# A two-layer hybrid trunk on one core: the layer head in parts behind weight splits, the spatial gating in two parts inside branch C

## The chip, the cores and the metric

The kernel runs on one core of one Trainium2 chip. Its engines are TensorE (PE), VectorE (DVE), ScalarE (ACT), GpSimd (POOL) and SyncE (SP); each works through its own queue in order. The metric is the device time of one execution in microseconds (us). Three runs of the kernel before took 1119.67, 1120.45 and 1121.61 us, median 1120.45. A time differs from that measurably from about 0.2% on, some 2.2 us.

## The reference

Input x is 512 tokens by 1024. Two layers, each a parallel mixer, then a final RMSNorm:

```
h    = rmsnorm(x, norm_g)
proj = h @ w_in            # aq ak av az | u vb | bz | cq ck cv cz | gl
A: 4 heads, differential causal attention; rmsnorm; * silu(az)
B: vb = layernorm(gelu(vb)); u = gelu(u)
   mixed = tril(sgu_w) applied to vb in chunks of 128 tokens, per group, + sgu_b
   yb = u * mixed * silu(bz)
C: 8 heads, three dilated windows merged by their log-sums; * silu(cz)
x    = x + (sum over branches of sigmoid(gl) * (y @ w_branch)) @ w_out
```

All is float32. The kernel keeps that precision by splitting: each operand is a high half (rounded) plus a low half, and a product is three matmuls (high by high, high by low, low by high).

## The kernel before, in words

Activations lie transposed, features on the partitions: `xh`/`xl` are the two halves of the normalised x, 8 tiles (kc) of 128 by 512. Weights stream from memory as `raw` tiles of 512 KB on SP's queue (two buffers). Each half of a `raw` tile is split: ScalarE rounds it to `whi` (L160), VectorE, or every fifth time GpSimd, takes the rest as `wlo` (L161). There are six `whi` and five `wlo` buffers. `proj_T` (L398 to L400) and `proj_M` (L423 to L425) consume them; a pair of outputs not listed in `EIGHT` goes by a scheme of seven products of half size (`seven`), which needs sums of weights (L180 to L183) and differences of x's blocks, `mh`/`ml` (`mixes`).

TensorE's memory holds two projection banks `ps_pj`, one double bank `ps_s` for scores, and four `ps_to` for transposes and products with the values.

`plan()` gives the order of the dense items of a layer: `vb`, `val A`, `val C`, `split`, `mix`, `pp A 0` (the head), then the items pulled while attention A runs, then those for attention C, then gates (`gl2`), branch products (`pb`) and the output. `vb` and the two `val` run on the unnormalised x (`xuh`, `xul`), with the norm applied to their outputs. Meanwhile in the head x is scaled (L556, eight VectorE instructions issued at once in `vb`), split to `xh`/`xl` (`split`, half of the low parts on GpSimd) and mixed (`mix`); the gelu and the statistics of `vb` also stand there. `pp A 0` is the first item that needs `xh`/`xl`.

While attention runs, its function calls `fill()` at fixed points, which pulls as much from the dense stream as a budget from `cost()` allows; `need()` forces an item that attention waits for. Scores (L828) of one step go into `ps_s`; VectorE subtracts and takes the maximum (L840), ScalarE exponentiates (L844) and normalises (L862), TensorE transposes (L868), the transposes are split (L403, L404) and multiplied with the values (L974). Each head has three steps (blocks 0 and 1, 2, 3). The spatial gating (`sgu`, L641 to L665) comes after attention C. Its weights `sgw` are loaded on ScalarE's queue. A scheduler fixes every engine's order at build time; weight splits and scores get high priority there.

Of the kernel before, what the change touches and what calls it, by code (L numbers as in the profile page):

```python
# [99 lines left out]
def hybrid_kernel(ctx: ExitStack, tc, xT, posr, wpack, tabs, cvec, pvec, rvec, lamv, sguw, outT):  # L100
# [366 lines left out]
    def mixes(blocks):  # L467

        for h in range(2):
            b11, b12, b21, b22 = blocks(h)  # L470

            def t2(tag, bufs=2):
                return t2k(tag, bufs, name="tm").rearrange("p (k c) -> p k c", k=2)

            m1, m2, m3, m4 = t2("t1"), t2("ob"), t2("sh"), t2("z", 5)
            V.tensor_tensor(out=m1, in0=b12, in1=b11, op=ALU.subtract)
            G.tensor_tensor(out=m3, in0=b22, in1=b12, op=ALU.subtract)
            V.tensor_tensor(out=m2, in0=b22, in1=m1, op=ALU.subtract)
            G.tensor_tensor(out=m4, in0=b21, in1=m2, op=ALU.subtract)
            for i, m in enumerate((m1, m2, m3, m4)):  # L480
                split(mh[:, i, 2 * h : 2 * h + 2, :], ml[:, i, 2 * h : 2 * h + 2, :], m)
# [46 lines left out]
    def layer(l, xu, parts):  # L528
# [13 lines left out]
        def i_vb():  # L542
# [18 lines left out]
            yield from proj_M(banks, xu.pair, {1: norm_sum, 4: scale})  # L561
            rst = norm["rst"]
            mv = sm.tile([P, 4, 2], F32, tag="mv", bufs=1, name="mv")
            rv = sm.tile([P, 4, 1], F32, tag="rv", bufs=1, name="rv")
            for tb in range(4):
                o = vb[:, tb, :]
                A.activation(out=o, in_=banks[tb], func=AF.Copy, scale=rst[:, tb : tb + 1])
# [550 lines left out]
```

## Time and profile before

| | before |
|---|---|
| median of three runs | 1120.45 us |
| profiled execution, whole | 1120.12 us |
| its span in the trace | 1118.4 us |
| TensorE busy | 1087.5 us, 97% |
| VectorE busy | 821.1 us, 73% |
| ScalarE busy | 597.5 us, 53% |
| GpSimd busy | 494.3 us, 44% |

The profiled execution's time exceeds its span by 1.7 us (start and end outside the trace) and lies 0.33 us below the median. Busy shares are averages over the whole span; what bounds a stage is read from the timeline and the waits of that stage. A matmul's duration overlaps the next one's, so the step from start to start tells its price. "[7.30 <-DVE wlo L161]" behind a row says that the engine was idle for 7.30 us before it and that VectorE's `wlo` at line 161 released it.

### The profile page before, as it was taken

The page shows a single profiled execution, that of the slowest core. Times are in us where ns is not written, and L with a number is a line of the kernel's source. Part 1 is how long each engine was busy: PE and PEld are TensorE (multiplying, and loading weights), DVE is VectorE, ACT ScalarE, POOL GpSimd, SP SyncE. Part 2 cuts the span into 40 slices and gives each one's busy share as a digit, 9 for nine tenths or more (in the row PEclk, how much of TensorE's full clock was granted, in tenths as well). Part 3 has the DMA queues.
Part 4 walks back from the last instruction along what each step waited for, and adds up shares of the span by engine and source line. Part 5 has one row for each costly group of instructions (what it writes and reads, how often), then busy time and mean ns, then how long its engine had stood idle before and what let it go on. Part 6 is the DMA issues. An engine that isn't in the chain of part 4 may idle for free.

```text
span 1118.4 us, 17917 instructions
## 1 busy us (share of the span) xinstructions
PE 1087.5 (97%) x6444; PEld 939.0 (84%) x6444; DVE 821.1 (73%) x1500; ACT 597.5 (53%) x1281; POOL 494.3 (44%) x438
## 2 busy tenths in 40 slices
PE   7799999999999999999999999999999999999996
PEld 5688888878888999998888888888788889999886
DVE  7775788566869888874559578885778797878643
ACT  6654565566765444443546546564758644444330
POOL 3312534432525756663334235525243357657431
PEclk9999999999999999999999999999999999999998
DMA  6243131221213323333622413122202132333433
GB/s 205 76 132 95 40 110 60 95 76 38 76 48 104 101 92 111 102 115 105 230 90 76 132 38 114 59 93 76 74 29 87 57 95 95 101 109 94 139 121 99
DMA packets 35064, 105.97 MB, mean 95 GB/s; under 512 B 4704, under 2 KB 7776, under 8 KB 34976
## 3 DMA queue, kind: packets, MB, share of 16 engines
q1 hardware_dynamic: 29936, 98.50, 27.9%
q10 hardware_dynamic: 5040, 6.34, 1.9%
q8 instruction: 51, 0.84, 0.3%
q14 instruction: 37, 0.30, 0.1%
HBM read 100.58 MB, written 4.24 MB: 94 GB/s over the span
## 4 chain that ended last, share of the span: by engine, by line
PE 84%; DVE 9%; DMA 2%; issue 2%; ACT 2%; POOL 1%; POOLq 0%; SPq 0%; DVEq 0%; ACTq 0%
PE ps_pj L398 15%; PE ps_pj L399 14%; PE ps_pj L400 14%; PE ps_to L398 8%; PE ps_to L399 8%; PE ps_to L400 8%; PE ps_s L828 3%; PE ps_to L868 2%; DVE wlo L161 2%; PE ps_to L974 2%; PE ps_to L425 2%; PE ps_to L423 2%; PE ps_to L424 2%; DMA raw<-in_wpack 2%; DVE xf L556 1%
## 5 line engine op out<-in xcount | busy, mean ns | idle before, releaser
L160 ACT ACTIVATE whi<-raw 128x512 fp32r<-128x512 f32 x316 | 193.1, 626 | 236.1 <-DMA raw<-in_wpack 106.8
L161 DVE TENSOR_TENSOR wlo<-raw,whi 128x512 fp32r<-128x512 f32 x261 | 220.2, 852 | 112.9 <-ACT whi L160 41.8
L398 PE MATMUL ps_pj<-xh,whi 128*128 128x512 f32 (+1 forms) x544 | 208.3, 383 | 1.1 <-DVE r L848 0.6
L400 PE MATMUL ps_pj<-xh,wlo 128*128 128x512 f32 (+1 forms) x544 | 205.9, 378 | 0.0
L399 PE MATMUL ps_pj<-xl,whi 128*128 128x512 f32 (+1 forms) x544 | 204.0, 375 | 0.0
L161 POOL TENSOR_TENSOR wlo<-raw,whi 128x512 fp32r<-128x512 f32 x55 | 78.6, 1429 | 129.0 <-ACT whi L160 32.5
L398 PEld LDWEIGHTS ps_pj<-xh,whi 128*128 128x128 f32 x544 | 102.5, 188 | 22.2 <-issue 3.7
L400 PEld LDWEIGHTS ps_pj<-xh,wlo 128*128 128x128 f32 x544 | 102.6, 189 | 17.9 <-issue 1.0
L399 PEld LDWEIGHTS ps_pj<-xl,whi 128*128 128x128 f32 x544 | 102.5, 189 | 17.8 <-issue 1.7
L161 DVE TENSOR_TENSOR wlo<-t,whi 128x512 fp32r<-128x512 f32 x88 | 91.4, 1056 | 21.1 <-ACT whi L160 18.4
L160 ACT ACTIVATE whi<-t 128x512 fp32r<-128x512 f32 x112 | 65.4, 624 | 57.8 <-DVE t L181 42.4
L398 PE MATMUL ps_to<-mh,whi 128*128 128x256 f32 x320 | 91.2, 285 | 1.8 <-ACT whi L160 1.3
L844 ACT ACTIVATE pr<-pr,nm 128x128 f32<-128x128 f32 (+3 forms) x128 | 70.6, 553 | 39.8 <-DVE nm L840 39.8
L400 PE MATMUL ps_to<-mh,wlo 128*128 128x256 f32 x320 | 90.4, 283 | 0.1
L399 PE MATMUL ps_to<-ml,whi 128*128 128x256 f32 x320 | 90.5, 283 | 0.0
L441 POOL TENSOR_TENSOR rsh<-rsh,sinr 128x512 f32<-128x512 f32 x32 | 42.0, 1311 | 105.5 <-DVE rsh L439 101.9
L840 DVE CUSTOM_DVE_ANT_0 pr<-ps_s,tab 128x128 f32<-128x128 f32 (+3 forms) x128 | 56.2, 484 | 22.1 <-PE ps_s L828 17.0
L400 PE MATMUL ps_to<-xh,wlo 128*128 128x256 f32 x240 | 67.9, 284 | 2.3 <-DVE wlo L161 2.1
L398 PE MATMUL ps_to<-xh,whi 128*128 128x256 f32 x240 | 67.9, 283 | 0.3 <-ACT whi L160 0.3
L399 PE MATMUL ps_to<-xl,whi 128*128 128x256 f32 x240 | 67.8, 283 | 0.0
L398 PEld LDWEIGHTS ps_to<-mh,whi 128*128 128x128 f32 x320 | 61.3, 192 | 3.7 <-ACT whi L160 2.4
L400 PEld LDWEIGHTS ps_to<-mh,wlo 128*128 128x128 f32 x320 | 61.2, 192 | 0.5 <-DVE wlo L161 0.3
(241 smaller groups left out, 2854.1 us busy)
## 6 DMA issues: line engine op xcount, KB each, us to landing
raw<-in_wpack SPq DMA_DIRECT2D x174, 512.0 KB
xf<-in_xT SPq DMA_DIRECT2D x8, 256.0 KB
xr<-in_xT ACTq DMA_DIRECT2D x8, 256.0 KB
x1d<-xf SPq DMA_DIRECT2D x8, 256.0 KB
raw<-in_wpack SPq DMA_DIRECT2D x4, 256.0 KB
xr<-x1d ACTq DMA_DIRECT2D x4, 256.0 KB
xr<-x1d ACTq DMA_DIRECT2D x8, 128.0 KB
out<-xf SPq DMA_DIRECT2D x8, 128.0 KB
```

What stands on the lines that cost most here:

```text
L160: A.activation(out=hi, in_=src, func=AF.Copy)
L161: (G if made[0] % LOMOD == 0 and made[0] > FIRST_G else V).tensor_tensor(out=lo, in0=src, in1=hi.bitcast(F32), op=ALU.subtract)
L398: T.matmul(ps, lhsT=wh, rhs=mh, start=first, stop=False)
L399: T.matmul(ps, lhsT=wh, rhs=ml, start=False, stop=False)
L400: T.matmul(ps, lhsT=wl, rhs=mh, start=False, stop=last)
L423: T.matmul(banks[tb], lhsT=mh_[:, ts], rhs=wh, start=kc == 0, stop=False)
L424: T.matmul(banks[tb], lhsT=ml_[:, ts], rhs=wh, start=False, stop=False)
L425: T.matmul(banks[tb], lhsT=mh_[:, ts], rhs=wl, start=False, stop=kc == KC - 1)
L441: G.tensor_tensor(out=sh, in0=sh, in1=sinr, op=ALU.mult)
L828: T.matmul(pss[:, m, at[i]], lhsT=q[HALF[m], a, qs], rhs=k[HALF[m], b, :W], start=t == 0, stop=t == 2,)
L840: V.tensor_tensor_reduce(out=o, in0=pss[:, m, at[i]], in1=tab[:, 0 if br == BR_A else 1, S - W :], op0=ALU.add, op1=ALU.min, scale=-0.125, ...
L844: A.activation(out=o, in_=o, func=AF.Exp, scale=-1.0, bias=nm[:, m : m + 1], accum_out=den[:, m : m + 1],)
```

## The change

Five things change. (1) The scaling and splitting of x is done one kc at a time after each kc of `val A`, the mixing after each kc of `val C`, each queued behind the newest weight split (`behind_weights`), all subtractions on VectorE. (2) `vb`'s gelu and statistics leave the head: four items `vbg` stand between the end of attention A's items and the middle of C's, `vbn` after `pp C 2`. (3) The lambda constants are computed at the end of layer 0's last mix; the loads of the gating weights stand behind weight splits in branch C. (4) `sgu` is split into `sgu 0` and `sgu 2`, inside C's items, uses `ps_pj` and writes back to `uz`; after C an item `yb` only splits the result. (5) There are six `wlo` buffers, and the last layer's sums of squares of the right half are on VectorE.

```diff
-    start = [("vb",), ("val", BR_A), ("val", BR_C), ("split",), ("mix",), ("pp", BR_A, 0)]
-    ... + [("vbn",), ("u2", 2), ("bz2", 0), ("pp", BR_C, 0)]
-    c = [("pp", BR_C, i) for i in range(1, 6)] + [("bz2", 2)]
+    start = [("vb",), ("val", BR_A), ("val", BR_C), ("pp", BR_A, 0)]
+    a += [("u2", 2), ("vbg", 0), ("bz2", 0), ("vbg", 1), ("pp", BR_C, 0), ("vbg", 2)]
+    c = [("pp", BR_C, 1), ("vbg", 3), ("pp", BR_C, 2), ("vbn",), ("sgu", 0), ("pp", BR_C, 3), ("bz2", 2), ("pp", BR_C, 4)]
+    c += [("sgu", 2), ("pp", BR_C, 5)]
-    end = gl[:1] + [("after", "C"), ("sgu",)] + gl[1:2]
+    end = gl[:1] + [("after", "C"), ("yb",)] + gl[1:2]
...
+    def behind_weights():
+        with tc.issue_after(newest[0]), tc.issue_after(newest[1]):
+            yield
...
-            lo = wp.tile([P, S], F32R, tag="wlo", bufs=NSLOT - 1, name="wlo")
+            lo = wp.tile([P, S], F32R, tag="wlo", bufs=NSLOT, name="wlo")
...
-                (V if kc == KC - 1 or self.first else G).tensor_tensor(out=self.ss[:, c], ...
+                (V if kc == KC - 1 or self.first or c.start else G).tensor_tensor(out=self.ss[:, c], ...
...
-                for kc in range(KC):
-                    xsc = xu.f[kc // 2][:, kc % 2, :]
-                    V.scalar_tensor_tensor(
-                        out=xsc, in0=xsc, scalar=ng[:, l, kc : kc + 1], in1=rbc, op0=ALU.mult, op1=ALU.mult
-                    )
...
-                gelu2(o, o)
-                V.bn_stats(out=st[:, tb, :], in_=o)
-                V.bn_aggr(out=mv[:, tb, :], in_=st[:, tb : tb + 1, :])
...
+        def prepare(kc):
+            with behind_weights():
+                xsc = xu.f[kc // 2][:, kc % 2, :]
+                V.scalar_tensor_tensor(
+                    out=xsc, in0=xsc, scalar=ng[:, l, kc : kc + 1], in1=norm["rbc"], op0=ALU.mult, op1=ALU.mult
+                )
+                if kc:
+                    split_x(kc - 1)
+        def mix(kc):
+            with behind_weights():
+                if kc == 0:
+                    split_x(KC - 1)
+                    norm["mix"] = mixes(xu.f)
+                next(norm["mix"])
+                if kc == KC - 1:
+                    next(norm["mix"])
+                    if l == 0:
+                        lambdas()
...
+        def i_sgu(g0):
+            vb, uz = sgu["vb"], sgu["uz"][g0 // 2]
+            if g0 == 0:
+                with behind_weights():
+                    nc.scalar.dma_start(out=sgw[0], in_=rvec[l : l + 1, :].partition_broadcast(P))
+                    nc.scalar.dma_start(out=sgw[1], in_=sguw[l])
...
+                pw = ps_pj()
+                T.matmul(pw, lhsT=ones, rhs=sgw[1], start=True, stop=True)
...
+            for i in range(2):
+                pm = ps_pj()
...
+                    out=uz[:, i, :], in0=ob, scalar=0.25, in1=uz[:, i, :], op0=ALU.mult, op1=ALU.mult
...
+        def i_yb():
+            for i in range(2):
+                split(yhl[BR_B][0][i], yhl[BR_B][1][i], sgu["uz"][i])
...
-            flat = {"vbn": 0.0}
+            flat = {"vbn": 0.0, "vbg": 0.0, "sgu": 2.0}
```

In the rows of order that follow, `xf` is x before the split, `tm` a difference of its blocks, `ml` and `xl` low halves.

VectorE's queue in layer 0's head, before, from the eight scalings on:

```order
L556 SCALAR_TENSOR_TENSOR xf<-xf,pv,rbc 128x512 x8
L569 BN_STATS st<-vb 128x6
L462 SCALAR_TENSOR_TENSOR vb<-gth,vb 128x512
L460 SCALAR_TENSOR_TENSOR gw<-gw,vb 128x512 x2
L404 TENSOR_TENSOR xl<-xf,xh 128x512 x3
L161 TENSOR_TENSOR wlo<-raw,whi 128x512
L404 TENSOR_TENSOR xl<-xf,xh 128x512
L570 BN_AGGR mv<-st 128x2
L161 TENSOR_TENSOR wlo<-raw,whi 128x512
L569 BN_STATS st<-vb 128x6
```

VectorE's queue in the same head now, from the last scaling on (the last kc of `val A` and the first of `val C`):

```order
L588 SCALAR_TENSOR_TENSOR xf<-xf,pv,rbc 128x512
L416 TENSOR_TENSOR xl<-xf,xh 128x512
L172 TENSOR_TENSOR wlo<-raw,whi 128x512
L497 TENSOR_TENSOR tm<-xf 128x512
L416 TENSOR_TENSOR xl<-xf,xh 128x512
L172 TENSOR_TENSOR wlo<-raw,whi 128x512
L497 TENSOR_TENSOR tm<-xf 128x512
L416 TENSOR_TENSOR ml<-tm,mh 128x512
L172 TENSOR_TENSOR wlo<-raw,whi 128x512
L497 TENSOR_TENSOR tm<-xf,tm 128x512
L416 TENSOR_TENSOR ml<-tm,mh 128x512
```

What stood in one go, the eight scalings and the gelu's steps ahead of the next `wlo`, now stands one kc at a time between the `wlo` of the weights, and the gelu and the statistics are not there.

TensorE's queue in layer 0's attention C, before, at head 1's first scores (blocks 0 and 1):

```order
L828 MATMUL ps_s<-k,q 128x128 x6
L828 MATMUL ps_s<-k,q 128x256 x6
L398 MATMUL ps_pj<-xh,whi 128x512
L399 MATMUL ps_pj<-xl,whi 128x512
L400 MATMUL ps_pj<-xh,wlo 128x512
L398 MATMUL ps_pj<-xh,whi 128x512
```

The same place now, from the last matmul of `pp C 2` on (`sgw` by `ones` is the gating's row sum, `sgw` by `vb` its product):

```order
L412 MATMUL ps_pj<-xh,wlo 128x512
L1010 MATMUL ps_to<-pth,vs 128x256
L1010 MATMUL ps_to<-ptl,vs 128x256
L1010 MATMUL ps_to<-pth,vs 128x256
L1010 MATMUL ps_to<-ptl,vs 128x256
L904 MATMUL ps_to<-ident,pr 128x128 x6
L864 MATMUL ps_s<-k,q 128x128 x6
L864 MATMUL ps_s<-k,q 128x256 x6
L671 MATMUL ps_pj<-sgw,ones 128x512
L685 MATMUL ps_pj<-sgw,vb 128x128 x4
L864 MATMUL ps_s<-k,q 128x384 x6
L904 MATMUL ps_to<-ident,pr 128x128 x8
```

Matmuls of a dense item stood behind the scores; now only attention's own work and `sgu 0` stand there.

ScalarE's queue at that place now (`th` reads the bank that `pp C 2` fills last):

```order
L880 ACTIVATE pr,den<-pr,nm 128x512 x2
L171 ACTIVATE whi<-raw 128x512
L664 DMA sgw<-in_rvec 128x512
L462 ACTIVATE th<-ps_pj 128x512
L665 DMA sgw<-in_sguw 128x512
L898 ACTIVATE pr<-pr,rd 128x512 x2
```

The load of the gating weights stands behind `th`; before it stood at the start of the program for layer 0.

TensorE's queue at head 3's last scores, before:

```order
L828 MATMUL ps_s<-k,q 128x512 x6
L868 MATMUL ps_to<-ident,pr 128x128 x3
L398 MATMUL ps_pj<-xh,whi 128x512
L399 MATMUL ps_pj<-xl,whi 128x512
L400 MATMUL ps_pj<-xh,wlo 128x512
L398 MATMUL ps_pj<-xh,whi 128x512
L399 MATMUL ps_pj<-xl,whi 128x512
L400 MATMUL ps_pj<-xh,wlo 128x512
L398 MATMUL ps_pj<-xh,whi 128x512
L974 MATMUL ps_to<-pth,vs 128x256
L399 MATMUL ps_pj<-xl,whi 128x512
L400 MATMUL ps_pj<-xh,wlo 128x512
```

The same place now (`mh` by `whi` is a piece of `gl A 0`, a gate by seven products):

```order
L864 MATMUL ps_s<-k,q 128x512 x6
L1010 MATMUL ps_to<-pth,vs 128x256
L1010 MATMUL ps_to<-ptl,vs 128x256
L1010 MATMUL ps_to<-pth,vs 128x256
L1010 MATMUL ps_to<-ptl,vs 128x256
L1010 MATMUL ps_to<-pth,vs 128x256
L904 MATMUL ps_to<-ident,pr 128x128 x3
L1010 MATMUL ps_to<-ptl,vs 128x256
L1010 MATMUL ps_to<-pth,vs 128x256
L1010 MATMUL ps_to<-ptl,vs 128x256
L904 MATMUL ps_to<-ident,pr 128x128 x3
L410 MATMUL ps_pj<-mh,whi 128x256
```

Dense matmuls of the eight-product kind stood between the instructions of attention; those (`bz2 2`, `gl B 0`) now come ahead of head 3's scores, and behind them only pieces of `gl A 0` are left.

## Rows read from the trace of the kernel before

**Rows 1.** The page: busy time of each engine over the span (share, instructions), and the chain that ended last by engine.

```profile
PE 1087.5 (97%) x6444; PEld 939.0 (84%) x6444; DVE 821.1 (73%) x1500; ACT 597.5 (53%) x1281; POOL 494.3 (44%) x438
...
PE 84%; DVE 9%; DMA 2%; issue 2%; ACT 2%; POOL 1%; POOLq 0%; SPq 0%; DVEq 0%; ACTq 0%
```

**Rows 2.** Busy microseconds of each engine in stretches of 10 us: stretch, its length, then PE, PEld, DVE, ACT, POOL (instructions in brackets), the granted TensorE clock (PEclk), DMA share, GB/s.

```profile
50.00:60.00 10.00, 3.52 (x8) 2.81 (x9) 10.00 (x14) 2.48 (x5) 3.48 (x3) 0.72 0.17 52
310.00:320.00 10.00, 10.00 (x67) 8.29 (x66) 7.07 (x23) 8.44 (x23) 3.75 (x6) 1.00 0.17 54
340.00:350.00 10.00, 8.30 (x66) 7.69 (x65) 9.94 (x19) 6.07 (x12) 3.71 (x2) 1.00 0.39 130
350.00:360.00 10.00, 8.99 (x67) 8.15 (x66) 10.00 (x13) 5.77 (x12) 6.34 (x4) 1.00 0.35 116
610.00:620.00 10.00, 9.59 (x43) 7.62 (x42) 7.93 (x14) 7.30 (x12) 4.54 (x3) 1.00 0.44 125
890.00:900.00 10.00, 7.97 (x49) 6.34 (x50) 10.00 (x16) 4.08 (x8) 4.05 (x3) 1.00 0.26 77
```

**Rows 3.** PE's waits over the whole span: what waited, for whom, us in total, times, longest.

```profile
PE ps_pj L425 <- DVE wlo L161: 7.3, 1, 7.3
```

**Rows 4.** TensorE's timeline at the head of layer 0, from the first matmul of `val A` (33.16) to the first of `pp A 0` (87.44): start, duration, engine, line, operation, tiles, shape, count, and in brackets the idle time before with its releaser.

```profile
33.16 0.39 PE L423 MATMUL ps_pj<-whi,xuh 128*128 128x512 f32 x1
33.39 0.39 PE L424 MATMUL ps_pj<-whi,xul 128*128 128x512 f32 x1
...
56.48 1.22 PE L425 MATMUL ps_pj<-wlo,xuh 128*128 128x512 f32 x2 [7.30 <-DVE wlo L161]
57.51 0.63 PE L425 MATMUL ps_s<-wlo,xuh 128*128 128x512 f32 x1
57.93 0.63 PE L423 MATMUL ps_s<-whi,xuh 128*128 128x512 f32 x1
...
60.92 0.57 PE L423 MATMUL ps_s<-whi,xuh 128*128 128x512 f32 x1
...
87.44 0.39 PE L398 MATMUL ps_pj<-xh,whi 128*128 128x512 f32 x1
```

**Rows 5.** VectorE's timeline in the same place.

```profile
40.49 8.51 DVE L556 SCALAR_TENSOR_TENSOR xf<-xf,pv,rbc 128x512 f32<-128x512 f32 x8
...
53.95 1.88 DVE L404 TENSOR_TENSOR xl<-xf,xh 128x512 fp32r<-128x512 f32 x3
55.75 0.68 DVE L161 TENSOR_TENSOR wlo<-raw,whi 128x512 fp32r<-128x512 f32 x1
```

**Rows 6.** VectorE by line and form between 33 and 62 us: count, busy us, mean ns of one, idle before.

```profile
L161 DVE TENSOR_TENSOR wlo<-raw,whi 128x512 fp32r<-128x512 f32 x6 | 4.0, 678 | 1.4 <-ACT whi L160 1.4
...
L404 DVE TENSOR_TENSOR xl<-xf,xh 128x512 fp32r<-128x512 f32 x4 | 2.6, 678 | 0.0
...
L476 DVE TENSOR_TENSOR tm<-xf 128x512 f32<-128x512 f32 x2 | 1.4, 676 | 0.0
```

**Rows 7.** TensorE's timeline at the end of branch C, in layer 0 (348 and 355) and layer 1 (899).

```profile
348.44 0.39 PE L400 MATMUL ps_to<-xh,wlo 128*128 128x256 f32 x1 [1.43 <-DVE wlo L161]
...
355.81 0.38 PE L398 MATMUL ps_to<-mh,whi 128*128 128x256 f32 x1 [0.99 <-ACT whi L160]
...
899.28 0.73 PE L398 MATMUL ps_pj<-yB,whi 128*128 128x512 f32 x2 [0.92 <-ACT yB L403]
```

**Rows 8.** The loading of layer 1's gating weights: its issue on ScalarE's queue, and the mask on GpSimd that waits for it.

```profile
359.06 0.33 ACTq L632 DMA_DIRECT2D sgw<-in_sguw  x1
...
361.72 0.86 POOL L636 TENSOR_SCALAR_AFFINE_SELECT sgw<-sgw 128x512 f32<-128x512 f32 x1 [3.25 <-DMA sgw<-in_sguw]
```

**Rows 9.** ScalarE in branch C by line between 225 and 345 us (columns as in rows 6; four heads): exponentials (L844) with their sums, normalising (L862), the high halves of the transposes (L403), and by form the `th` of a gate (L450).

```profile
L844 ACT ACTIVATE pr<-pr,nm 128x128 f32<-128x128 f32 (+3 forms) x32 | 17.6, 551 | 4.8 <-DVE nm L840 4.8
...
L862 ACT ACTIVATE pr<-pr,rd 128x128 f32<-128x128 f32 (+3 forms) x32 | 16.1, 552 | 2.6 <-DVE rd L848 2.6
L403 ACT ACTIVATE pth<-ps_to 128x128 fp32r<-128x128 f32 (+3 forms) x32 | 12.9, 430 | 8.2 <-PE ps_to L868 5.7 <-POOL ptl L952 2.3
L844 ACT ACTIVATION_READ_ACCUMULATOR pr<-pr,nm 128x1 f32 x32 | 6.0, 187 | 0.0
...
L450 ACT ACTIVATE th<-ps_pj 128x512 f32<-128x512 f32 x5 | 2.9, 582 | 0.0
```

**Rows 10.** TensorE in branch C: twelve matmuls of scores, and eight of 128 columns, in one go each.

```profile
310.96 0.96 PE L828 MATMUL ps_s<-k,q 64*128 64x128 f32 x12
...
352.58 1.05 PE L655 MATMUL ps_s<-sgw,vb 128*128 128x128 f32 x8
```

**Rows 11.** The first 30 us: two idle times of TensorE, and the loading of a function table on ScalarE.

```profile
19.68 0.49 PE L423 MATMUL ps_to<-whi,xuh 128*128 128x512 f32 x1 [0.55 <-ACT whi L160]
...
23.01 1.19 PE L425 MATMUL ps_to<-wlo,xuh 128*128 128x512 f32 x4 [1.22 <-DVE wlo L161]
...
23.80 1.28 ACT L350 ACT_TABLE_LOAD   x1
```

**Rows 12.** The end of the program: the last sum of squares on GpSimd and the matmul that waits for it.

```profile
1108.24 0.72 POOL L276 TENSOR_TENSOR ssum<-ssum,sq 128x256 f32<-128x256 f32 x1 [4.55 <-ACT sq L272]
...
1109.02 0.38 PE L375 MATMUL ps_s<-ones,ssum 128*128 128x1 f32 x2 [1.00 <-POOL ssum L276]
```

More of the change, by code (lines that the diff above doesn't have):

```diff
@@ L1 @@
 import math
-from contextlib import ExitStack
+from functools import partial
+from contextlib import ExitStack, contextmanager
 import concourse.bass as bass
@@ L275, in square @@
                     return
-                (V if kc == KC - 1 or self.first else G).tensor_tensor(out=self.ss[:, c], in0=self.ss[:, c], in1=sq[:, c], op=ALU.add)
+                (V if kc == KC - 1 or self.first or c.start else G).tensor_tensor(out=self.ss[:, c], in0=self.ss[:, c], in1=sq[:, c], op=ALU.add)
         def pair(self, kc):
@@ L465, in hybrid_kernel, with mixes, rest @@
     LT, RT = slice(0, 256), slice(256, 512)
-    def mixes(blocks):
-        for h in range(2):
[L470 to L481, printed above, removed]
+    def mixes(xf):
+        todo = []
+        def rest():
+            for h, i, m in todo:
+                split(mh[:, i, 2 * h : 2 * h + 2, :], ml[:, i, 2 * h : 2 * h + 2, :], m)
+            todo.clear()
+        for h in range(2):
+            a, b = xf[h], xf[2 + h]
+            b11, b12, b21, b22 = a[:, :, LT], a[:, :, RT], b[:, :, LT], b[:, :, RT]
+            m1, m2, m3, m4 = (
+                t2k(tag, bufs, name="tm").rearrange("p (k c) -> p k c", k=2)
+                for tag, bufs in (("t1", 2), ("ob", 2), ("sh", 2), ("z", 5))
+            )
+            for i, m, x1, x2 in ((0, m1, b12, b11), (2, m3, b22, b12), (1, m2, b22, m1), (3, m4, b21, m2)):
+                V.tensor_tensor(out=m, in0=x1, in1=x2, op=ALU.subtract)
+                rest()
+                todo.append((h, i, m))
+                yield
+        rest()
+        yield
     def seven(bank=ps_to):
@@ L560, in i_vb @@
             banks = [ps_to() for _ in range(4)]
[L561 to L562 removed]
+            yield from proj_M(banks, xu.pair, {1: norm_sum, 4: spread})
             mv = sm.tile([P, 4, 2], F32, tag="mv", bufs=1, name="mv")
             rv = sm.tile([P, 4, 1], F32, tag="rv", bufs=1, name="rv")
+            sgu["norm"] = st, mv, rv
             for tb in range(4):
[L566 to L570 removed]
@@ L571, in i_vb @@
-            V.tensor_scalar(out=rv, in0=mv[:, :, 1:2], scalar1=4.0 * EPS, scalar2=None, op0=ALU.add)
-            G.tensor_tensor(out=rv[:, :, 0], in0=rv[:, :, 0], in1=mhalf, op=ALU.pow)
-            sgu["norm"] = mv, rv
-        def i_split():
-            for kc in range(KC):
-                split(xh[:, kc, :], xl[:, kc, :], xu.f[kc // 2][:, kc % 2, :], G if kc in XLG else V)
-            return
-            yield
-        def i_mix():
-            def blocks(h):
-                a, b = xu.f[h], xu.f[2 + h]
-                return a[:, :, LT], a[:, :, RT], b[:, :, LT], b[:, :, RT]
-            mixes(blocks)
-            return
-            yield
+                A.activation(out=vb[:, tb, :], in_=banks[tb], func=AF.Copy, scale=norm["rst"][:, tb : tb + 1])
@@ L654, in i_sgu @@
                 for tb in range(4):
                     T.matmul(
[L656 to L657 removed]
+                        pm[:, tb * P : (tb + 1) * P], lhsT=vb[:, tb, gs], rhs=wc[:, gs], start=True, stop=True
                     )
@@ L675, in i_val @@
                 banks = [ps_pj(), ps_pj(), ps2[:, 0, :], ps2[:, 1, :]]
-                yield from proj_M(banks, xu.pair, {})
+                yield from proj_M(banks, xu.pair, {kc: partial(prepare, kc) for kc in range(KC)})
                 for tb in range(4):
@@ L682, in i_val @@
             banks = [ps_to() for _ in range(4)]
-            yield from proj_M(banks, xu.pair, {})
+            yield from proj_M(banks, xu.pair, {kc: partial(mix, kc) for kc in range(KC)})
             val[br] = v = att.tile([P, 4, 8, P], F32R, tag="vs", name="vs")
@@ L802, in layer @@
         fns = {
-            "vb": i_vb, "split": i_split, "mix": i_mix, "vbn": i_vbn, "after": i_after, "u2": i_u2, "bz2": i_bz2, "sgu": i_sgu, "val": i_val, "pp": i_pp, "gl2": i_gl2, "pb": i_pb, "out": i_out,
+            "vb": i_vb, "vbg": i_vbg, "vbn": i_vbn, "after": i_after, "u2": i_u2, "bz2": i_bz2, "sgu": i_sgu, "yb": i_yb, "val": i_val, "pp": i_pp, "gl2": i_gl2, "pb": i_pb, "out": i_out,
         }
```

83 lines of the change are left out of this document (44 added, 39 removed).

## The prediction

> **What bounds the kernel now.** First the page: TensorE is busy for 1087.5 of 1118.4 us and carries 84% of the chain that ended last [rows 1]. The matmuls that the change leaves are the same ones (the same products of the same sizes), so it can only win or lose in the 30.9 us in which TensorE is idle and in the stretches at its lower clock. Second, busy time by stretch, to find these places: 50 to 60 us has 3.52 busy and a granted clock of 0.72; 340 to 360 lacks 1.70 and 1.01 us, together 2.71; 890 to 900 lacks 2.03; 610 to 620 lacks 0.41 [rows 2]. Third, TensorE's waits name the largest: 7.3 us at once for a `wlo` of VectorE [rows 3]. Fourth, the timeline there. VectorE has scaled x for 8.51 us from 40.49 on and then does gelu and splits until 55.75, when the awaited `wlo` comes up [rows 5]; TensorE starts again at 56.48, and its matmuls step by 0.42 us until about 60.9, against 0.23 at 33.16 [rows 4]. So the lower of the two clock levels (1.2 GHz) is granted behind the gap of 7.30 us: the price of the gap goes on for 4.4 us after it. Behind the gaps of 1.43 and 0.99 us in branch C [rows 7] the clock stays at 1.00 [rows 2].
>
> **The change part by part. Layer 0's head.** From the first matmul of `val A` (33.16) to the first of `pp A 0` (87.44) it takes 54.28 us [rows 4]. In between stand 2 x 96 matmuls; at 0.23 they take 44.2. The difference of 10.1 us is what can go: 7.3 of idle time, some 2.0 of lower clock (4.4 us in which steps of 0.42 do the work of 0.23), the rest small. Does the new order remove it? For each kc TensorE has 12 matmuls, 2.76 us. VectorE has a `wlo`, a scaling and an `xl` or a `wlo`, a `tm` and an `ml`: three instructions of about 0.68 [rows 6], 2.05 us. ScalarE has two, of some 0.6 by an instruction of the same size [rows 9]. Both keep up, and the order puts each `wlo` ahead of the additions that could delay it, with six split weights in advance. The late one next would be the last mix, ahead of `pp A`'s seven-product relatives only, which come later. What weighs on this is the duration: the eight scalings took 8.51 us, 1.06 each [rows 5], where those `wlo`s and `tm`s that ran beside an idle GpSimd took 0.68. In the new order GpSimd has no subtraction in the head, so I take 0.68; the other end is a rival below. The Trainium skill ("SBUF — State Buffer", section "SBUF: two separate sides") says that a VectorE instruction with two memory inputs and a GpSimd instruction lock one port pair against each other for a whole instruction; by that rule too the slow duration goes with GpSimd's work, and the sum would stay as it is, while without it VectorE's 3.2 us per kc would be the bound. Gain: 10.0, between 3 and 10.1.
>
> The gelu of `vb` and its statistics (four times three instructions of 0.68 [rows 6], some 8 us of VectorE) move to the end of attention A and into C. They are hidden where VectorE has slack: 310 to 320 us shows it busy for 7.07 of 10 with TensorE at 10.00 [rows 2]. I cost it at nothing; without cover it would delay a `wlo` by one instruction at a time, under 1 us in all. The constants: TensorE's idle times of 0.55 and 1.22 at 19.68 and 23.01 wait for ScalarE's splits around the loads of function tables, of which one (1.28 us) moves away [rows 11]; two loads of 256 KB leave the early rush, while `tab` (512 KB) goes ahead of one `raw` tile on SP's queue. I take 1.0 of the 1.8 as gain, between -1 and 1.8. The head of layer 1 loses its 0.41 [rows 2]. The final sum waits 1.00 for GpSimd's addition of 0.72 [rows 12]; on VectorE it can gain 0.2. The sixth `wlo` buffer costs nothing and gives nothing by itself. Gains together: 10.0 + 1.0 + 0.4 + 0.2 = 11.6.
>
> **The gating inside C, first part.** The order shows that after the last matmul of `pp C 2` (call it T) no dense matmul stands until `pp C 3`, whose first one needs a bank that `sgu 0` holds: both projection banks are its own. The row sum of the gating weights waits for their load, issued on ScalarE behind `th`, which reads what ends at T: 0.58 [rows 9], with 0.1 to start, so T + 0.7. Such a load was issued at 359.06 and its mask started at 361.72: 2.66 us, and the mask takes 0.65 to 0.86 [rows 8]. So the row sum starts at about T + 4.1. TensorE has until then four products with values, six transposes and twelve scores, by [rows 10] 10 x 0.13 + 0.96, some 2.0 (a little is pipelined away). It waits 2.1 us, and scores, transposes and products queued behind it wait too; nothing else on TensorE may pass. Per layer 2.1, between 1.3 (a faster load) and 5 (each of the two gating products also waits for VectorE's softmax pieces), so 4.2 for both layers. The second part (`sgu 2`) has dense matmuls around it and its weights at hand: 0.2 per layer, 0.4. Before, the gating stood where TensorE had dense pieces, and cost no more than the idle times of [rows 7].
>
> **The end of C.** With `sgu` counted at 2.0 in `cost()`, and `bz2 2` brought forward, the stream is spent sooner: head 3's last scores are followed by transposes and products alone, then by pieces of `gl A 0` whose split weights stand behind attention's work on ScalarE. TensorE's work from head 3's first scores to its last product with values I count from the order at 11.7 us. ScalarE's work for one head is (17.6 + 16.1 + 12.9 + 6.0) / 4 = 13.2 [rows 9], and splits of branch outputs and weights stand between. So at least 1.5 us are idle per layer. Following the order of ScalarE and VectorE instruction by instruction with these rows I get 16.3 us to the last product, 4.6 idle, and 2.5 more until the branch products of B, which wait for `yb`'s splits: 7.1. I take 4.6, since the pieces of `gl A 0` should cover `yb`. Before, the same place lost 2.71 and 2.03 [rows 2]. Loss: 2 x 4.6 - 4.7 = 4.5, between -1.7 and 9.5.
>
> **Sum.** The profiled execution takes 1120.12, its span 1118.4 and 1.7 around it. 1120.12 - 11.6 + 4.2 + 0.4 + 4.5 = 1117.6. The median of the runs lies 0.33 above that execution, so I forecast 1117.9: most of the head's gain is given back inside branch C.
>
> **Rivals.** *A: the gain stays.* The gating's wait is 1.3 and the end of C has only the 1.5 that ScalarE's work forces, so that also the old idle time there shrinks: -11.6 + 2.6 + 0.4 - 1.7 = -10.3, 1110. For it: TensorE had no idle time between 310 and 320, in the midst of C, where VectorE has slack [rows 2]. Against it: there dense matmuls filled the gaps, and the order shows that they are elsewhere now.
>
> *B: slower, the dense stream runs dry in C.* One mechanism: with no dense matmul behind the scores, the whole softmax of a head lies bare on TensorE, at `sgu 0` for 5 us and at the end for 7.1. Then -11.6 + 10 + 0.4 + 9.5 = +8.3, 1128.7. It decides from the point where C's idle time passes 16 us in all (the 11.6 gained and the 4.7 of before), 8 per layer. For it: the hand count gives 7.1. Against it: every step of that count must be as late as I have it. If a gap there also lowers the clock, as the one of 7.30 did, 2.0 us come on top for each. The Trainium skill ("TensorE: Matmul & The Clock Gate", section "Why this matters for your kernels") warns that idle gaps between bursts of matmuls put TensorE back to half clock; the trace agrees behind 7.30 us and shows no fall behind 1.43, and for a gap of 2 to 4 us no row here decides. By the rule with one fall per layer B is 1133.
>
> *C: VectorE becomes the head's bound.* At 1.06 for each of three instructions [rows 5] it needs 3.2 us per kc against 2.76: 16 x 0.44 = 7.0 come back, 1125. For it: the scalings did take that long. Against it: GpSimd was at work beside them, and is not any more.
>
> *D: the change does not do what it says.* If the delayed instructions only move the wait for `wlo` from `val A` to `pp A 0`, head and C each change by little and the time is the same, about 1120.
>
> **How the numbers follow.** Forecast 0.50, with its own range of 1113 to 1123; A 0.17; B 0.20; C 0.08; D 0.05. The range over 8 of 10 reaches from somewhat below A's time to B's: 1108.5 to 1128.5. About 0.2%, 2.2 us, is what a measurement of this kernel tells from no change. Of the forecast's half, 0.27 lies below 1118.2, 0.21 within, 0.02 above. Faster: 0.27 + 0.17 = 0.44. Within 0.2%: 0.21 + D's 0.05 + 0.04 from the edges of B and C = 0.30. Slower: 0.02 + 0.18 + 0.06 = 0.26.
>
> **What would show it.** In the trace of the changed kernel: no idle time over 1 us and a clock of 1.00 between 33 and 80 us, `pp A 0` starting about 10 us sooner (near 76); in each layer an idle time of about 2 us on TensorE, released by GpSimd's mask, before the gating's row sum; and 4 to 5 us of idle time between head 3's scores and the first branch product, put down to ScalarE. The prediction is wrong if the head still has a gap, or if branch C's idle time per layer is under 3 or over 10 us.

## The result and the profile after

The changed kernel takes 1133.94 us (median of four, 1133.38 to 1134.41), the kernel before beside it 1120.06: ratio 1.0123, interval 1.011 to 1.0135. It is slower, where 1117.9 was forecast, and outside the range. The profiled execution has a span of 1132.3 us, 13.9 more than before. First the page: busy time of each engine, and the chain that ended last by engine.

```profile
PE 1092.5 (96%) x6444; PEld 946.8 (84%) x6444; DVE 823.9 (73%) x1515; ACT 599.7 (53%) x1277; POOL 474.7 (42%) x419
...
PE 85%; DVE 5%; ACT 3%; issue 3%; DMA 2%; POOL 1%; POOLq 0%; DVEq 0%; ACTq 0%
```

Against [rows 1] TensorE is busy 5.0 us longer with the same 6444 matmuls, and it is idle 39.8 instead of 30.9 us, 8.9 more. These two are the 13.9; since the matmuls are the same, I read the 5.0 us as steps at the lower clock. Where they lie shows in TensorE's timeline. In the changed kernel, at the first matmul of `pp A 0`, of layer 1, and of `pp A 0` in layer 1:

```profile
75.11 0.39 PE L410 MATMUL ps_pj<-xh,whi 128*128 128x512 f32 x1
...
561.29 0.39 PE L435 MATMUL ps_to<-whi,xuh 128*128 128x512 f32 x1
...
628.42 0.39 PE L410 MATMUL ps_pj<-xh,whi 128*128 128x512 f32 x1
```

Before, at the first matmul of layer 1:

```profile
561.89 0.39 PE L423 MATMUL ps_to<-whi,xuh 128*128 128x512 f32 x1
```

`pp A 0` starts at 75.11, before at 87.44 [rows 4]: the head and the first 30 us gain 12.3. But layer 1 starts at 561.29, against 561.89 before: between the two places 11.7 us are lost. Layer 1's head gains another 0.7 (67.13 from its start to `pp A 0`, before 67.85); from there to the end 15.2 are lost. -12.3 + 11.7 - 0.7 + 15.2 is the 13.9. Busy time by stretch (columns as in [rows 2]):

```profile
50.00:60.00 10.00, 10.00 (x46) 8.29 (x45) 6.88 (x11) 6.92 (x12) 0.00 (x0) 1.00 0.33 107
240.00:250.00 10.00, 8.49 (x50) 6.73 (x51) 6.37 (x25) 7.63 (x23) 0.72 (x2) 0.83 0.18 56
330.00:340.00 10.00, 6.00 (x39) 5.64 (x38) 6.91 (x14) 7.39 (x16) 5.58 (x8) 0.83 0.00 1
340.00:350.00 10.00, 7.11 (x52) 6.14 (x50) 9.94 (x14) 8.88 (x15) 3.03 (x3) 1.00 0.33 106
350.00:360.00 10.00, 9.33 (x44) 7.95 (x45) 6.69 (x9) 2.70 (x5) 4.46 (x4) 0.83 0.28 75
790.00:800.00 10.00, 6.04 (x34) 4.38 (x34) 6.31 (x24) 8.28 (x24) 2.17 (x6) 0.78 0.46 160
890.00:900.00 10.00, 7.27 (x40) 6.32 (x40) 6.69 (x12) 6.66 (x12) 3.22 (x3) 0.83 0.19 58
900.00:910.00 10.00, 7.45 (x47) 7.24 (x48) 9.88 (x13) 5.93 (x10) 4.40 (x3) 0.83 0.14 49
```

At 50 to 60 us, where TensorE had 3.52 busy and a clock of 0.72 [rows 2], it is full at 1.00. The new holes lie in branch C, around 240, 335 and 350 in layer 0, 797, 890 and 902 in layer 1, and all of these stretches but one (340 to 350) have a clock of 0.78 to 0.83. TensorE's waits name the releasers (columns as in [rows 3]):

```profile
PE ps_pj L410 <- ACT whi L171: 9.1, 4, 4.0
PE ps_pj L671 <- POOL sgw L666: 6.0, 2, 3.7
...
PE ps_pj L410 <- DVE zs L529: 4.9, 3, 2.2
PE ps_pj L412 <- DVE wlo L172: 1.9, 1, 1.9
```

The `wlo` wait of 7.3 us is gone; in its place stand ScalarE's `whi` at the end of C, the mask of the gating weights (on GpSimd), and `zs`, a sum of VectorE in the seven-product scheme. The two largest places in the timeline are these. The first is the gating's row sum (L671) in both layers, with the last dense matmul before it in layer 0 (at 236.78; this is T, as in the prediction) and the first one behind it in both:

```profile
236.78 0.40 PE L412 MATMUL ps_pj<-xh,wlo 128*128 128x512 f32 x1
...
238.24 0.95 PE L864 MATMUL ps_s<-k,q 64*128 64x128 f32 x12
241.51 1.13 PE L671 MATMUL ps_pj<-sgw,ones 128*128 128x512 f32 x2 [2.31 <-POOL sgw L666]
...
250.85 0.48 PE L410 MATMUL ps_pj<-xh,whi 128*128 128x512 f32 x1
...
797.10 2.07 PE L671 MATMUL ps_pj<-sgw,ones 128*128 128x512 f32 x2 [3.72 <-POOL sgw L666]
...
807.40 0.48 PE L410 MATMUL ps_pj<-xh,whi 128*128 128x512 f32 x1
```

Layer 0 has 14.07 us without a dense matmul, layer 1 16.74 (its T is 790.66). The load that the mask waits for, in layer 1:

```profile
791.29 0.56 ACTq L665 DMA_DIRECT2D sgw<-in_sguw  x1
...
796.41 0.64 POOL L666 TENSOR_SCALAR_AFFINE_SELECT sgw<-sgw 128x512 f32<-128x512 f32 x1 [4.59 <-DMA sgw<-in_sguw]
```

From issue to mask it takes 5.12 us; in layer 0 it takes 3.59 (issue at 237.22, mask at 240.81). The second place is the end of C in layer 0, from the last transposes to the branch products of `yB`:

```profile
330.56 0.49 PE L904 MATMUL ps_to<-ident,pr 128*128 128x128 f32 x3
335.04 0.58 PE L410 MATMUL ps_pj<-mh,whi 128*128 128x256 f32 x1 [4.00 <-ACT whi L171]
...
344.36 0.36 PE L410 MATMUL ps_pj<-xh,whi 128*128 128x256 f32 x1 [0.40 <-DVE eb L529]
...
346.46 0.47 PE L410 MATMUL ps_pj<-yB,whi 128*128 128x512 f32 x1 [0.44 <-ACT whi L171]
347.44 0.39 PE L410 MATMUL ps_to<-xh,whi 128*128 128x256 f32 x1 [0.51 <-ACT whi L171]
...
350.67 0.50 PE L410 MATMUL ps_pj<-yB,whi 128*128 128x512 f32 x1 [2.20 <-DVE zs L529]
```

The gap of 4.00 us ends when a `whi` of `gl A 0` is ready. ScalarE, VectorE and GpSimd there:

```profile
330.11 1.16 ACT L415 ACTIVATE y<-yf 128x512 fp32r<-128x512 f32 x2
...
334.36 0.63 ACT L171 ACTIVATE whi<-t 128x512 fp32r<-128x512 f32 x1 [0.93 <-DVE t L194]
```

```profile
330.90 2.36 DVE L416 TENSOR_TENSOR y<-yf,y 128x512 fp32r<-128x512 f32 x2
...
333.65 0.67 DVE L194 TENSOR_TENSOR t<-t,raw 128x512 f32<-128x512 f32 x1
```

```profile
331.18 1.53 POOL L193 TENSOR_TENSOR t<-raw 128x512 f32<-128x512 f32 x1 [0.17 <-issue]
```

`whi` waits for a sum of weights `t` on VectorE (L194), which stands behind two splits of a branch output taking 2.36 us in all: 0.69 for the first and 1.75 for the second, which runs beside GpSimd's sum. That sum itself starts only at 331.18. No dense matmul is left to cover that chain. The second large wait, 2.20 us, stands in front of a product of `yB` and ends with `zs`, which stands in VectorE's queue right behind the second of `yb`'s splits (1.21 us from 349.06). Layer 1 shows the gap of 4.00 us as well, with 3.98.

### The profile page after: what moved, and what is told of

Same layout as the page of the kernel before. It is cut to its first block, busy times and chain, and to the rows that moved or that the text cites. A ratio compares the mean times of both kernels' runs of the same rounds, so it can differ in the third digit from the quotient of the medians.

```text
span 1132.3 us, 17831 instructions
## 1 busy us (share of the span) xinstructions
PE 1092.5 (96%) x6444; PEld 946.8 (84%) x6444; DVE 823.9 (73%) x1515; ACT 599.7 (53%) x1277; POOL 474.7 (42%) x419
## 4 chain that ended last, share of the span: by engine, by line
PE 85%; DVE 5%; ACT 3%; issue 3%; DMA 2%; POOL 1%; POOLq 0%; DVEq 0%; ACTq 0%
PE ps_pj L410 14%; PE ps_pj L412 14%; PE ps_pj L411 14%; PE ps_to L412 8%; PE ps_to L410 8%; PE ps_to L411 8%; PE ps_to L435 3%; PE ps_s L864 3%; PE ps_to L437 3%; PE ps_to L436 3%; PE ps_to L904 2%; PE ps_to L935 1%; DVE wlo L172 1%; PE ps_to L1010 1%; DMA raw<-in_wpack 1%
## 5 line engine op out<-in xcount | busy, mean ns | idle before, releaser
L172 DVE TENSOR_TENSOR wlo<-t,whi 128x512 fp32r<-128x512 f32 x88 | 82.5, 952 | 19.0 <-ACT whi L171 18.5
```

The costliest lines, as they stand in the source:

```text
L172: r = (G if on_g else V).tensor_tensor(out=lo, in0=src, in1=hi.bitcast(F32), op=ALU.subtract)
```

## The experiments

Theory 1: all of the loss comes from dense matmuls that no longer stand beside attention in branch C. Theory 2: it comes from the work that left the head and now loads ScalarE and VectorE in C. To compare stages I use the time from the first product with values of attention C to the first output product: 265.4 us (layer 0) and 265.5 (layer 1) before, 277.6 and 282.4 in the changed kernel, so 29.0 us are lost there in both layers together. Its two ends in layer 0, before and in the changed kernel:

```profile
247.52 0.28 PE L974 MATMUL ps_to<-pth,vs 128*128 128x256 f32 x1
...
512.93 0.39 PE L398 MATMUL ps_to<-mg,whi 128*128 128x512 f32 x1
```

```profile
234.71 0.28 PE L1010 MATMUL ps_to<-pth,vs 128*128 128x256 f32 x1
...
512.33 0.39 PE L410 MATMUL ps_to<-mg,whi 128*128 128x512 f32 x1
```

Runs of one group stood on one chip beside the kernel before, and each ratio is to that: 1121.42 us for the first four runs below, 1122.02 for the second group (filled gap, six buffers, and the two first ones with the gating weights in attention A), 1120.47 for the last (the two repeats, five buffers, gelu in the head).

**Head alone.** The gating back behind attention C in the form of before, the rest as changed.

```diff
-    c = [("pp", BR_C, 1), ("vbg", 3), ("pp", BR_C, 2), ("vbn",), ("sgu", 0), ("pp", BR_C, 3), ("bz2", 2), ("pp", BR_C, 4)]
-    c += [("sgu", 2), ("pp", BR_C, 5)]
+    c = [("pp", BR_C, 1), ("vbg", 3), ("pp", BR_C, 2), ("vbn",)] + [("pp", BR_C, i) for i in range(3, 6)] + [("bz2", 2)]
-    end = gl[:1] + [("after", "C"), ("yb",)] + gl[1:2]
+    end = gl[:1] + [("after", "C"), ("sgu",)] + gl[1:2]
```

> The new head (with vb's gelu still spread over attention A and C, six wlo buffers, late constants) and the old place of the gating, behind attention C, with bz2 2 back as the last item of C. Theory 1 (all of the loss comes from dense matmuls missing beside attention in branch C): the head's 12.3 + 0.7 us stay and C costs what it did before, so 1120 - 13 = 1107 us, and no idle time of TensorE over 1.5 us after 30 us. Theory 2 (the work moved out of the head, gelu and statistics of vb, is what loads ScalarE and VectorE in C): the time stays above 1120, with TensorE idle in C as in the changed kernel.

1110.89 us, ratio 0.9911 (0.9896 to 0.9926). The stage in C takes 266.3 and 267.7. Nearly all of the loss is gone with the old places of the gating and of `bz2 2`, though `vb`'s gelu is still in C: theory 2 does not explain it. But 10.5 us are gained, not 13: with the loads of the gating weights among the first transfers again `pp A 0` starts at 77.0, not 75.1, and C keeps 0.8 and 2.1 us more than before.

**Gating alone.** The head of before, but with six `wlo` buffers, and the gating in two parts in C.

```diff
-    start = [("vb",), ("val", BR_A), ("val", BR_C), ("pp", BR_A, 0)]
+    start = [("vb",), ("val", BR_A), ("val", BR_C), ("split",), ("mix",), ("pp", BR_A, 0)]
...
-                yield from proj_M(banks, xu.pair, {kc: partial(prepare, kc) for kc in range(KC)})
+                yield from proj_M(banks, xu.pair, {})
```

> The head of before (scaling in one go, gelu of vb in the head, constants early) with the gating in two parts inside C. Theory 1: C loses its 12 us in layer 0 and 15 in layer 1 as in the changed kernel, the head gains nothing: 1120 + 27 = 1147 us. Theory 2: without the gelu in C the gating fits in, 1120 to 1125 us.

1140.81 us, ratio 1.0168 (1.015 to 1.0186). The stage in C takes 278.8 and 278.1, 13 us more than before in each layer, without `vb`'s gelu in it. TensorE at the head's gap, and at the end of C:

```profile
57.83 0.73 PE L439 MATMUL ps_pj<-wlo,xuh 128*128 128x512 f32 x2 [3.05 <-DVE wlo L173]
...
344.80 0.39 PE L412 MATMUL ps_pj<-mh,whi 128*128 128x256 f32 x1 [4.00 <-ACT whi L172]
...
360.15 0.80 PE L412 MATMUL ps_pj<-yB,whi 128*128 128x512 f32 x1 [2.19 <-DVE zs L547]
```

The same 4.00 and 2.19 us stand at the end of C as in the changed kernel, which again speaks against theory 2. Here the row sum does not wait for its mask: softmax's waits of 0.63 and 0.59 us (layer 0) and 1.21 (layer 1) come first. So C can lose 13 us per layer without that wait. The whole is not 1147: the head's gap is 3.05 us, not 7.30, though a new one of 2.33 comes at 34.62, where a step of the norm waits for VectorE. The six `wlo` buffers led to the run with six buffers below.

**Gating weights early.** The loads are free to be issued as soon as their buffers are.

```diff
-                with behind_weights():
-                    nc.scalar.dma_start(out=sgw[0], ...
-                    nc.scalar.dma_start(out=sgw[1], ...
+                nc.scalar.dma_start(out=sgw[0], ...
+                nc.scalar.dma_start(out=sgw[1], ...
```

> The changed kernel, only that the loads of the gating weights may be issued as early as their buffers are free. Theory 1a (the load behind th makes the gap at the first gating matmul): the idle times of 2.3 and 3.7 us there and the half clock behind them (1.7 and 2.7) go, 1134 - 10 = 1124 us. Rival 1b (the place is bare of dense matmuls anyway, the next wait takes over): 1130 to 1134 us, with new idle times of 1 to 3 us at the gating products or the scores.

1130.75 us, ratio 1.0084 (1.0069 to 1.0099): 3 to 4 us less than the changed kernel and in the range of rival 1b, with smaller waits than it had. TensorE in layer 0's gating:

```profile
242.56 2.02 PE L684 MATMUL ps_pj<-sgw,vb 128*128 128x128 f32 x16 [0.64 <-DVE sgw L673]
...
246.94 0.39 PE L1009 MATMUL ps_to<-pth,vs 128*128 128x256 f32 x1 [0.78 <-ACT pth L415]
```

The wait for the mask is gone; 0.64 and 0.78 us of waits for VectorE and ScalarE took part of its place (1.00 and 0.68 in layer 1), and the clock stays at 1.00 there. The stretch without a dense matmul is still 12.0 and 12.2 us: the place is bare whether the weights come early or late. In layer 0, where `pp A 0` also starts 1.5 us later with the loads among the first transfers, nothing is won by layer 1's start (561.4).

**Dense item last.** Only the order of C's items.

```diff
-    c = [("pp", BR_C, 1), ("vbg", 3), ("pp", BR_C, 2), ("vbn",), ("sgu", 0), ("pp", BR_C, 3), ("bz2", 2), ("pp", BR_C, 4)]
-    c += [("sgu", 2), ("pp", BR_C, 5)]
+    c = [("pp", BR_C, 1), ("vbg", 3), ("pp", BR_C, 2), ("vbn",), ("sgu", 0), ("pp", BR_C, 3), ("pp", BR_C, 4)]
+    c += [("sgu", 2), ("pp", BR_C, 5), ("bz2", 2)]
```

> The changed kernel, only the order of items in C altered: C3, C4, sgu 2, C5, and bz2 2 last (it was between C3 and C4). Theory 1 (the end of C is bare because the dense items ahead of C5 are forced before head 3's scores): the idle times of 7.6 and 7.9 us at the end of C fall back to about the 2.7 and 2.0 of before, with 4 us less at half clock: 1134 - 14 = 1120 us. Rival 2 (the end is late because ScalarE is, with yb's splits of 1024 columns): 1131 to 1134 us, the idle time is still there.

1116.35 us, ratio 0.9957 (0.9942 to 0.9971): about 18 us less than the changed kernel (1.0123), by the place of one item. All idle times over 0.3 us at the end of C, in both layers:

```profile
340.82 0.47 PE L410 MATMUL ps_pj<-yB,whi 128*128 128x512 f32 x1 [0.44 <-DVE zs L529]
...
344.75 0.38 PE L410 MATMUL ps_to<-mh,whi 128*128 128x256 f32 x1 [0.94 <-ACT whi L171]
...
891.06 0.38 PE L410 MATMUL ps_to<-mh,whi 128*128 128x256 f32 x1 [1.30 <-ACT whi L171]
```

Instead of 7.55 and 7.85 us they are 1.38 and 1.30. So theory 1 holds for the end of C: `yb`'s splits, which are still there, cost little where a dense item covers them. The change had brought `bz2 2` ahead of `C 4` and `C 5`, which head 3 needs; so it was forced before head 3's scores. The stage in C now takes 268.9 and 272.1 us; what is left over before stands mostly at the gating, whose waits of 2.25 and 3.74 us are still there.

**Filled gap.** Constant matmuls ahead of the row sum, into the same bank; the row sum overwrites them.

```diff
                 pw = ps_pj()
+                for _ in range(6):
+                    T.matmul(pw, lhsT=ones, rhs=cosr, start=True, stop=True)
                 T.matmul(pw, lhsT=ones, rhs=sgw[1], start=True, stop=True)
```

> The changed kernel with six matmuls of constants (ones by the cosine table) into the bank of the gating's row sum, ahead of it, whose result the row sum overwrites; the wait for the gating weights stays as it is. They take about 2.6 us per layer, the idle times there are 2.31 and 3.72. Theory 1c (the clock's fall behind the gap costs some 1.7 and 2.7 us beside the gap itself): granted clock 1.00 behind the row sum in layer 0 at least, and 2 to 4 us less, 1130 to 1132. Rival (only the idle time counts): 1134 or up to 2 us more.

1135.8 us, ratio 1.0128 (1.0113 to 1.0143), no faster than the changed kernel's 1.0123: by the time alone the rival's number. The sizing was wrong: each of the six is two passes of 0.43 us, together 5.2 us per layer against gaps of 2.31 and 3.72. Still the run separates clock and wait. Busy time by stretch, and TensorE at the row sum and at the next dense matmul, in layer 0:

```profile
240.00:244.00 4.00, 4.00 (x20) 2.00 (x19) 2.39 (x11) 2.23 (x9) 0.65 (x1) 1.00 0.37 131
244.00:248.00 4.00, 4.00 (x29) 2.99 (x28) 2.80 (x8) 2.94 (x10) 0.00 (x0) 1.00 0.00 0
```

```profile
244.11 1.02 PE L674 MATMUL ps_pj<-sgw,ones 128*128 128x512 f32 x2
...
251.77 0.50 PE L411 MATMUL ps_pj<-xh,whi 128*128 128x512 f32 x1
```

The clock is 1.00. From the row sum to the next dense matmul it takes 7.66 us (layer 1: 7.67), in the changed kernel 9.34 and 10.30 for the same matmuls (241.51 to 250.85, 797.10 to 807.40). So the fallen clock costs 1.7 and 2.6 us behind these gaps; the added matmuls then took back what that saved.

**Six buffers in the kernel before.** One line.

```diff
-            lo = wp.tile([P, S], F32R, tag="wlo", bufs=NSLOT - 1, name="wlo")
+            lo = wp.tile([P, S], F32R, tag="wlo", bufs=NSLOT, name="wlo")
```

> The kernel before with one line changed: six buffers for the low halves of weights (five before). The prediction had it at nothing. In the gating-alone run, which has six, the gap in layer 0's head was 3.05 us, against 7.30. If the sixth buffer did that (one more split weight stands ahead of the eight scalings, 12 matmuls of 0.23 = 2.7 us, and the clock may hold): 1120 - 4 = 1116 us or a little less. If it was the shift of other instructions: 1119 to 1121.

1113.77 us, ratio 0.993 (0.9915 to 0.9946), more than expected. The head's gap of 7.30 us became two:

```profile
54.14 0.50 PE L423 MATMUL ps_to<-whi,xuh 128*128 128x512 f32 x1 [2.52 <-ACT whi L160]
...
57.64 1.22 PE L425 MATMUL ps_pj<-wlo,xuh 128*128 128x512 f32 x2 [2.07 <-DVE wlo L161]
```

The head gains 2.8 us (`pp A 0` at 84.7); the rest comes in small pieces along both layers (layer 1 starts 3.6 us sooner, its first output product 7.1). Once more, in the last group:

> The kernel before with six buffers for low halves, once more, beside the next kernel on one chip. As before: ratio 0.993, 1113.8 us.

1114.69 us, ratio 0.9941 (0.9928 to 0.9953).

**Dense item last, gating weights in attention A.** The dense-item-last version, with the loads of the gating weights and their mask moved to `vbg 0`, behind weight splits in attention A.

> The dense-item-last version with the loads of the gating weights and their mask issued behind weight splits in attention A (at vbg 0) instead of at the gating. Theory 1 (two bare places, the wait for the weights and the end of C): the idle times of 2.25 and 3.74 and the half clock behind them (about 4 us) go too, but as in the early-weights run some 1.5 us per layer of waits for VectorE remain: 1116.4 - 7 = 1109 us. Rival (bare attention there anyway, the weights do not matter): 1113 to 1116.

1111.25 us, ratio 0.9909 (0.9892 to 0.9925), some 5 us less than with the loads at the gating (0.9957), between the two expectations. The stage in C takes 266.8 and 270.1, against 266.3 and 267.7 in the head-alone version: with both bare places mended, the gating inside C is still no faster than behind it. By the stage times of these single traces, of the 29.0 us lost in C 19.0 go with the place of `bz2 2`, 4.1 with the loads, about 3 with the gating's place itself, and about 3 are left in the head-alone version.

**Head alone, gating weights in attention A**, twice, first in the second group:

> The head-alone version with the gating weights loaded behind weight splits in attention A (at vbg 0), not at the program's start. If the two loads of 256 KB among the first transfers make TensorE's remaining idle time of 1.10 at 22.4 us there: 1110.9 - 1 = 1109.9 us. If not: 1110.9.

1110.22 us, ratio 0.99 (0.9879 to 0.9921); the idle time of 1.10 us at 22.4 is gone, one of 0.36 at 37.7 came. The time cannot be told from the 0.9911 of the head-alone version. Then in the last group:

> The head-alone version with the gating weights loaded in attention A, once more, beside the six-buffer version. If the head's order adds to the buffer: 3 us below it, about 1110 us (2.5 + 2.1 us of idle time and half clock in layer 0's head are what is left there). If the order only repeats what the buffer gives: equal within 1 us.

1108.55 us, ratio 0.9893 (0.9879 to 0.9906), against 0.9941 for the six buffers alone beside it. The intervals do not overlap: what this version changes beside the buffer (the head's order above all, but also the place of the gelu and of the loads) adds 5 to 6 us.

**Head alone, five buffers.**

> The head-alone version with five buffers for low halves instead of six. The sixth buffer alone gave 8 us to the kernel before. If the new order of the head carries its gain by itself (no long stretch of VectorE between weight splits any more, so five suffice): within 2 us of the head-alone version's 1110.9. If the buffer carries it and the order adds little: 1116 to 1120.

1112.85 us, ratio 0.9931 (0.9917 to 0.9944). The head-alone version without the sixth buffer gains 7.6 us; its head has no gap (`pp A 0` at 77.5). Buffer and order each mend the same gap, the buffer in part, so their gains do not add.

**Gelu in the head.** The head-alone version with the four `vbg` right behind `vb`.

```diff
-    start = [("vb",), ("val", BR_A), ("val", BR_C), ("pp", BR_A, 0)]
+    start = [("vb",), ("vbg", 0), ("vbg", 1), ("vbg", 2), ("vbg", 3), ("val", BR_A), ("val", BR_C), ("pp", BR_A, 0)]
```

> The head-alone version with vb's gelu and statistics back in the head, right behind vb (some 8 us of VectorE), the scaling and mixing still one kc at a time. If the eight scalings in one go were the trouble: within 1 us of the head-alone version, 1110.9, and no gap in the head. If the gelu belonged to it: 1113 to 1116, with an idle time of 1 us or more in val A.

1106.5 us, ratio 0.9875 (0.9862 to 0.9889), the fastest of all, 14 us under the kernel before. Busy time by stretch in its head:

```profile
40.00:50.00 10.00, 9.95 (x45) 7.90 (x44) 9.46 (x20) 6.45 (x12) 0.35 (x1) 1.00 0.15 51
50.00:60.00 10.00, 10.00 (x46) 8.29 (x45) 8.18 (x15) 8.16 (x15) 1.64 (x1) 1.00 0.42 133
60.00:70.00 10.00, 10.00 (x46) 8.29 (x45) 10.00 (x18) 7.64 (x14) 0.00 (x0) 1.00 0.40 129
```

TensorE is full, though VectorE does gelu, statistics and scaling there. The six-buffer version of the kernel before, with the gelu there too and x's scaling, splitting and mixing in one go, kept 2.52 and 2.07 us. So the gap goes with that, and not with the gelu. The idle times of 1.11, 0.67 and 0.46 us that the head-alone version has at 825 to 829, for VectorE's `wlo` and `ptl`, are gone; the stage in C takes 266.2 and 263.8 us, against 266.3 and 267.7. So the gelu in A and C was not free: theory 2 holds for some 4 us in layer 1's C.

## Why the prediction was wrong

Branch C was put at 9.1 us of loss (4.2 + 0.4 + 4.5) and lost 29.0. What failed is how the waits in C were priced, not where they were expected. By the prediction's own sign (C's idle time per layer over 10 us) it is wrong too: the idle times over 0.3 us there add up to 11.25 us in layer 0 and 12.87 in layer 1.

**The head: right, and a little small.** Head and first 30 us were put at 11.0 and gave 12.3, layer 1's head 0.7 instead of 0.4. Rival C falls: VectorE's scalings took 0.745 us each in the new head, its splits 0.69, not 1.06. That 1.06 was an average: in the trace before five of the eight scalings took 0.75 us, and the three that ran beside a GpSimd subtraction 1.78. For the early idle times the prediction named the loads of function tables; the runs show that the loads of the gating weights matter. The head-alone version, with these among its first transfers, waits 1.10 us at 22.44 although a table load (23.80 before) stands only at 83.13; the gating-alone version has table loads at 18.34 and 23.25 but its gating weights later, and no such wait. "The sixth `wlo` buffer costs nothing and gives nothing by itself" was false: alone it gave 6 to 8 us.

**The gelu "at nothing": wrong.** VectorE's slack was read from one stretch (310 to 320 [rows 2]). The runs with it in C and in the head differ by ratios of 0.9911 (0.9896 to 0.9926) and 0.9875 (0.9862 to 0.9889).

**The gating's wait: right in place, too small.** The step put 2.1 us per layer. Layer 0 has 2.31, in part by luck: its load took 3.59 us from issue to mask, where the 2.66 of [rows 8] was taken, but TensorE's scores also ended later, at T + 2.4 instead of T + 2.0, and the load did not wait for `th` to run (issue at T + 0.44, `th` at T + 1.9). Layer 1 has 3.72, because its load, issued at 791.29, let the mask start at 796.41, 5.1 us later. The sum priced the wait alone and put what follows it at nothing. The next dense matmul came at T + 14.07 and T + 16.74; with the weights early it still came at T + 12.0 and T + 12.2, so the bare place itself is the larger part of this stretch. The lower clock behind the gap (1.7 and 2.6 us) was in a rival only.

**The end of C: the count was right, the choice from it wrong.** Counting the queues gave 7.1 us, and I took 4.6, "since the pieces of `gl A 0` should cover `yb`". Measured, by the idle times over 0.3 us: 4.00 + 0.40 + 0.44 + 0.51 + 2.20 = 7.55 in layer 0, 3.98 + 0.34 + 0.71 + 1.94 + 0.88 = 7.85 in layer 1. The pieces could not cover it, as their own weights were late: the first gap ends with a `whi` of `gl A 0`, and ScalarE could start it only when VectorE's sum `t` was done. The prediction had put this wait down to ScalarE. The 2.5 us counted for `yb`'s splits came as well: the largest wait behind the first gap is 2.20 us for `zs` behind such a split in layer 0, and 1.94 us in layer 1, there for a `wlo` of a gate that itself took 1.76 us. The second part of the gating was put at 0.2 per layer; 1.39 and 1.30 us appear at a sum of the seven-product scheme there.

**The clock.** The forecast had none of it. The idle time grew by 8.9 us over the whole span, and the 5.0 us more of busy time came although the head's 2.0 us at the lower clock went, so some 7.0 us in C. Rival B's mechanism happened, and its time with one fall of the clock per layer, 1133, is close to the measured 1133.94, but that is partly luck: there were three falls per layer, behind smaller gaps at the gating than B had assumed. The prediction's sentence that gave this time drew on the Trainium skill ("TensorE: Matmul & The Clock Gate", section "Why this matters for your kernels"), which warns of idle gaps between bursts of matmuls. The trace agrees that the clock falls behind gaps, but shorter ones than that section warns of were enough here: it was under 1.00 behind gaps of 1.94, 2.20 and 2.31 us, and 1.00 behind the 1.39 at 304.48.

Not tried: what part of the 4 us at the end of C would go by reordering VectorE's queue alone.

## What to carry to other kernels

Where attention is covered by a stream of dense matmuls, what counts is which dense items are left when its last head comes: an item listed ahead of one that this head needs is forced out early, and here one place in a list was worth about 18 us. If a count along the queues gives a time, discount it only for a reason that the queues themselves show, and add the lower clock to each gap as a term of the sum. Try the one-line part of a change by itself: a sixth buffer alone gave 6 to 8 us, and the rewritten head, which gave 10 to 12 with it, gave 7.6 without.
